# The down stage of a SwiGLU kernel takes its memory where gate/up leaves it, and starts loading inside the last gate/up product group

## The chip, the cores and the metric

The kernel runs on one core of one Trainium2 chip. The number that counts is the device time of one execution in microseconds (us). Inside the core TensorE (PE in the profile) multiplies matrices, VectorE (DVE) and ScalarE (ACT) do elementwise work, GpSimd (POOL) does elementwise work on SBUF alone, and SyncE (SP) issues all the DMAs named here. Each engine works through its own list of instructions in order and waits on semaphores of the others.

## The reference, cut to what matters

The whole is one layer of a streaming encoder: a mixer (SSD and band attention), then SwiGLU. Only the second half matters here, for 1,024 prompt frames and 32 sample frames, with 1,024 model columns and 2,816 hidden columns.

```
f = rmsnorm(x, norm_ffn_g)
x = x + (silu(f @ w_gate) * (f @ w_up)) @ w_down
```

## The kernel before, in words

All products use operands split into a high and a low float32r part, and three matmuls each (high by high, low by high, high by low). Gate/up and down both use a seven-product form of Strassen's scheme.

**Gate/up** goes over 11 pairs `n` of hidden blocks, and for each pair over gate (`w` = 0) and up (`w` = 1): 22 groups of seven products. `prep` loads two weight blocks `raw` (three buffers in pool `wp`), splits them on ACT and DVE and forms their sums on POOL; the results stand in `whi`/`wlo` (five buffers each). `quad` (L973) runs the seven products into four wide PSUM buffers and adds them into pieces of one large SBUF tile `sc`; its helper `product` (L963) issues 24 matmuls (L970). The B operands are `fA` (first and third product) and five tiles `T2, T1, T3, B22, T4` of pool `tq`. `use_up` (L999) multiplies up by the silu of gate and stores the 32 sample columns to `asm_d` in DRAM (L1003); `keep_acts` (L1019) stores the hidden activations to `act_d` in DRAM: seven operands, each split on ACT (L1012) and DVE (L1013) into two pieces that are used in turn, two stores each (L1015).

**Down** has 24 tiles. The first chunk of four tiles uses pair 0 alone, five further chunks use two pairs each (1 and 2, 3 and 4, to 9 and 10). A tile is 128 rows by two halves; it reads its activations (`load_act`, L1049), runs seven products of three matmuls per pair (L1123) and adds each into one of seven accumulators `Z` (L1128). `prep_down` (L1075) prepares one pair's weights: eight small matmuls with the sample activations `asm` (L1079), an add into `x2s`, then splits on ACT (L1091) and DVE (L1092) and sums on POOL (L1096 to L1100) into `chi`/`clo` (three buffers) and `bhi`/`blo` (nine buffers, three per pair). POOL's sums work in place on the raw weights, so they wait for the small matmuls that read these.

The down stage's pool `pd` is opened when gate/up's pools `hp`, `wp` and `tq` are closed, so it lies on their memory. All its loads stand in the program after the last `keep_acts`. The residual x enters as the first value of three accumulators (L1108, 1 MB each) and, in the chunk before the last, by an add on POOL. `load_act(tiles_[m + 2])` stands ahead of tile m, with three two-pair buffers.

The order on each engine is not the order in the source: a scheduler with a time model places each instruction in its engine's list. DMAs on SP use eight completion semaphores in turn, so each also waits for the DMA eight places earlier. What moves is therefore read from the lists.

Of the kernel before, what the change touches and what calls it, by code (L numbers as in the profile page):

```python
# [43 lines left out]
def build(tc, a):  # L44
# [856 lines left out]
    tq = pool("tq", stack=stT)  # L901
# [129 lines left out]
    work = [(w, n) for n in range(NF // 2) for w in range(2)]  # L1031
    ops = prep(*work[0])
    for k, (w, n) in enumerate(work):
        cur, ops = ops, prep(*work[k + 1]) if k + 1 < len(work) else None
        quad(cur, acts if w else gates, use_up(n) if w else use_gate)
        if w:
            keep_acts(n)
    stT.close()
    pvs.close()
    stH.close()  # L1040

    pd = pool("pd")
    pz = pool("pz", space=PSUM)
# [18 lines left out]
    load_raw(0)  # L1065
    load_raw(1)
    asm = pd.tile([P, NF, NS], F32, name="asm")
    nc.sync.dma_start(asm, asm_d)
    Z = pd.tile([P, 7, 4, 512], F32, name="Z")

    def bank1():
        return pz.tile([P, 512], F32, tag="z", bufs=8, name=nm("ps_z"))

    def prep_down(n):

        pb = bank1()
        for k in range(2):
            for g in range(4):
                nc.tensor.matmul(pb[32 * g:32 * g + 32, 0:256], lhsT=asm[:, 2 * n + k, :],  # L1079
# [181 lines left out]
```

## Time and profile before

| what | us |
|---|---|
| median of three runs (lowest, highest) | 1389.52 (1388.25, 1394.1) |
| the profiled execution | 1384.95 |
| its span, first to last instruction | 1383.2 |
| gate/up's last product ends, from the span's start | 1118.86 |
| first matmul of the down stage | 1145.62 |

Rows of stretches give the stretch and its length, then the busy time of each engine with its number of instructions, the clock that was granted to TensorE as a share of full speed, the mean busy share of the DMA engines and what they moved in GB/s. Rows of the chain of waits give start, length and what the chain passed through; the chain is followed back from the last instruction, so what stands in it set the end. A matmul's own duration is longer than the distance to the next, since matmuls are pipelined.

### The profile page before, as it was taken

What the parts mean: (1) busy time and instruction counts of PE and PEld (TensorE: products, weight loads), DVE (VectorE), ACT (ScalarE), POOL (GpSimd) and SP (SyncE); (2) the same over time, 40 slices, a digit from 0 to 9 for tenths busy, and PEclk for the clock granted to TensorE, in tenths of its full rate; (3) what the DMA queues carried; (4) which work ended last, traced back from release to release, by engine and by line L of the source; (5) the groups of instructions that cost most, each with busy time, mean ns of one, the idle gap of its engine ahead of it and who ended that gap; (6) DMA issues with size and microseconds to landing.
All of it is one profiled execution on the core that took longest, in us unless ns stands there. A gap on an engine that the chain in (4) does not pass through costs nothing.

```text
span 1383.2 us, 23748 instructions
## 1 busy us (share of the span) xinstructions
PE 1283.8 (93%) x9260; PEld 1171.9 (85%) x9260; DVE 901.3 (65%) x1271; ACT 502.2 (36%) x865; POOL 600.2 (43%) x495
## 2 busy tenths in 40 slices
PE   5999999878998999997799999999999937999998
PEld 4999999868887788786799999999999935787877
DVE  6356537685757556666777666776766636666896
ACT  7244332322346444544533333333333315111210
POOL 7142258986645101302344435445435315232585
PEclk9999999988999999999999999999999978999999
DMA  7174351445387986654144444554444368766654
GB/s 272 70 229 133 95 177 59 152 161 171 111 255 220 312 266 208 217 172 149 51 138 133 130 145 133 168 154 128 130 144 137 109 197 323 283 224 229 253 187 175
DMA packets 200848, 241.99 MB, mean 175 GB/s; under 512 B 25088, under 2 KB 162368, under 8 KB 200736
## 3 DMA queue, kind: packets, MB, share of 16 engines
q1 hardware_dynamic: 200736, 240.47, 53.2%
q8 instruction: 73, 1.20, 0.4%
q14 instruction: 39, 0.32, 0.1%
HBM read 149.44 MB, written 90.99 MB: 174 GB/s over the span
## 4 chain that ended last, share of the span: by engine, by line
PE 66%; DVE 7%; POOL 6%; issue 6%; DMA 6%; ACT 2%; SPq 1%; DVEq 0%; ACTq 0%; POOLq 0%
PE ps_w L970 32%; PE ps_z L1123 11%; PE ps_mm L153 3%; PE ps_mm L154 3%; PE ps_mm L155 3%; PE ps_mm L162 2%; PE ps_mm L160 2%; PE ps_mm L161 2%; DVE Z L1128 2%; PE ps_mm L734 2%; PE ps_t L717 1%; POOL dm L541 1%; PE ps_s L695 1%; PE ps_s L699 1%; DMA mx<-mix_d 1%
## 5 line engine op out<-in xcount | busy, mean ns | idle before, releaser
L970 PE MATMUL ps_w<-T,whi 128*128 128x264 f32 x1408 | 231.3, 287 | 7.9 <-ACT T L918 7.3
L970 PEld LDWEIGHTS ps_w<-T,whi 128*128 128x128 f32 x1408 | 196.9, 190 | 8.6 <-ACT T L918 7.7
L1123 PE MATMUL ps_z<-bhi,at 128*128 128x512 f32 x528 | 168.2, 393 | 3.9 <-ACT bhi L1091 3.9
L978 DVE TENSOR_TENSOR sc<-sc,ps_w 128x528 f32<-128x528 f32 x154 | 105.4, 698 | 83.3 <-PE ps_w L970 81.0
L153 PE MATMUL ps_mm<-whi,hT_hi 128*128 128x256 f32 (+1 forms) x512 | 149.5, 292 | 5.1 <-ACT hT_hi L227 3.5
L155 PE MATMUL ps_mm<-whi,hT_lo 128*128 128x256 f32 (+1 forms) x512 | 148.9, 291 | 0.5 <-DVE hT_lo L228 0.5
L154 PE MATMUL ps_mm<-wlo,hT_hi 128*128 128x256 f32 (+1 forms) x512 | 148.9, 291 | 0.0
L970 PE MATMUL ps_w<-T,wlo 128*128 128x264 f32 x704 | 144.2, 286 | 0.0
L139 POOL TENSOR_TENSOR wlo<-raw,whi 128x1024 fp32r<-128x1024 f32 (+1 forms) x32 | 80.7, 2531 | 131.5 <-ACT whi L138 130.0
L1128 DVE TENSOR_TENSOR Z<-ps_z,Z 128x512 f32<-128x512 f32 x152 | 101.9, 687 | 44.1 <-PE ps_z L1123 37.4
L1123 PEld LDWEIGHTS ps_z<-bhi,at 128*128 128x128 f32 x528 | 99.5, 189 | 26.3 <-ACT bhi L1091 5.2
L946 ACT CAST whi<-raw 128x1024 fp32r<-128x1024 f32 x88 | 82.9, 944 | 101.6 <-PE ps_w L970 85.2
L970 PE MATMUL ps_w<-fA,whi 128*128 128x264 f32 x704 | 115.6, 287 | 0.0
L947 DVE TENSOR_TENSOR wlo<-raw,whi 128x1024 fp32r<-128x1024 f32 x88 | 107.1, 1218 | 6.0 <-ACT whi L946 3.4
L1013 DVE TENSOR_TENSOR sc<-sc 128x512 fp32r<-128x512 f32 x77 | 74.6, 980 | 54.8 <-DMA act_d<-sc 29.7
L970 PEld LDWEIGHTS ps_w<-T,wlo 128*128 128x128 f32 x704 | 109.8, 190 | 0.0
L153 PEld LDWEIGHTS ps_mm<-whi,hT_hi 128*128 128x128 f32 x512 | 99.8, 195 | 6.8 <-ACT hT_hi L227 3.9
L1123 PE MATMUL ps_z<-blo,at 128*128 128x512 f32 x264 | 103.4, 393 | 1.1 <-DVE blo L1092 1.0
L155 PEld LDWEIGHTS ps_mm<-whi,hT_lo 128*128 128x128 f32 x512 | 99.9, 195 | 1.8 <-DVE hT_lo L228 1.2
L154 PEld LDWEIGHTS ps_mm<-wlo,hT_hi 128*128 128x128 f32 x512 | 99.7, 195 | 0.3
L970 PEld LDWEIGHTS ps_w<-fA,whi 128*128 128x128 f32 x704 | 98.6, 190 | 0.0
L1012 ACT CAST sc<-sc 128x512 fp32r<-128x512 f32 x77 | 46.8, 621 | 122.6 <-DVE sc L1002 77.7
(268 smaller groups left out, 2928.8 us busy)
## 6 DMA issues: line engine op xcount, KB each, us to landing
act_d<-sc SPq DMA_DIRECT2D x154, 256.0 KB, 2.9
at<-act_d SPq DMA_DIRECT2D x20, 1792.0 KB, 7.1
raw<-in_wgu_dram SPq DMA_DIRECT2D x44, 512.0 KB, 3.5
raw<-in_wd_dram SPq DMA_DIRECT2D x22, 512.0 KB, 4.5
x<-in_xp_dram SPq DMA_DIRECT2D x16, 512.0 KB, 6.7
q<-qst_d SPq DMA_DIRECT2D x32, 256.0 KB, 4.8
mx<-mix_d SPq DMA_DIRECT2D x16, 512.0 KB, 4.5
raw<-in_wq_dram SPq DMA_DIRECT2D x14, 512.0 KB, 5.1
```

Source lines behind the costliest of these rows:

```text
L139: (eng or nc.gpsimd).tensor_tensor(lo, raw, hi, op=ALU.subtract)
L153: nc.tensor.matmul(ps_, lhsT=lh, rhs=rh, start=start, stop=False)
L154: nc.tensor.matmul(ps_, lhsT=lh, rhs=rl, start=False, stop=False)
L155: nc.tensor.matmul(ps_, lhsT=ll, rhs=rh, start=False, stop=stop)
L946: nc.scalar.copy(out=t[0][:, 0:w], in_=src)
L947: nc.vector.tensor_tensor(t[1][:, 0:w], src, t[0][:, 0:w], op=ALU.subtract)
L970: nc.tensor.matmul(out[:, h, :], lhsT=A[x][:, kb, :], rhs=B[:, y, kb, h * Q:(h + 1) * Q], start=(n == 0), stop=(n == len(terms) - 1))
L978: add = lambda o, x, y: nc.vector.tensor_tensor(o, x, y, op=ALU.add)
L1012: nc.scalar.copy(out=hi.bitcast(F32R), in_=src)
L1013: nc.vector.tensor_tensor(lo.bitcast(F32R), src, hi, op=ALU.subtract)
L1123: nc.tensor.matmul(pb, lhsT=at[:, k, q, x, :], rhs=bops[n0 + k][name][y], start=(i == 0), stop=(i == len(terms) - 1))
L1128: eng.tensor_tensor(o, x, y, op=ALU.add)
```

## The change

Memory of the down stage is laid into places that gate/up leaves one after another, instead of a pool opened after all of it.

- `tq` moves to the other side of SBUF; `hp` and `wp` stay open to the end. The four activation places are now slices of `fA`, which the last group frees after its third product; a fifth (`at5`) is added after gate/up. A two-pair tile takes two of the five places, each loaded by a DMA of its own.
- Weights of a pair go into the `whi`/`wlo` buffers (five) and into `sd`, which lies on `sc` (four more places). `chi`/`clo` lie in the `raw` buffers of `wp`.
- Pair 0 is loaded and prepared, and its small matmuls run, within the last group of seven products, with a copy of its sample columns in `mixS`. The first four tiles' activations are loaded from the third product of that group on.
- The residual no longer fills three accumulators at the start. The first chunk writes all seven (four products by ACT, three by DVE), and POOL adds the residual later: two per tile in the chunk of pairs 3 and 4, one per tile in the chunk of pairs 5 and 6, and one, as before, in the chunk of pairs 7 and 8.
- `prep_next` places the second pair of a chunk behind the fourth tile of the chunk before; the loads of tile m + 2 stand behind tile m.

```diff
-    tq = pool("tq", stack=stT)
+    tq = pool("tq", stack=stT, side="right")
...
+    fA_f = fA.rearrange("p s k c -> p (s k c)")
+    at_slots = [fA_f[:, k * 4 * H:k * 4 * H + 7 * 2 * P] for k in range(4)]
+    b_slots, c_slots = [], []
+    at_turn, b_turn = [0], [0]
+    asm0 = mixS[:, 0:2, :]
     def load_act(key):
         n0, r, tp = key
-        at = pd.tile([P, r, 7, 2, P], F32R, tag="at", bufs=3, name=nm("at"))
-        nc.sync.dma_start(at.bitcast(F32), act_d[n0:n0 + r, :, tp].rearrange("n p q s c -> p n q s c"))
-        ats[key] = at
-    chunks_ = [(0, 1)] + [(n, 2) for n in range(1, NP, 2)]
-    tiles_ = [(n0, r, tp) for n0, r in chunks_ for tp in range(4)]
-    load_act(tiles_[0])
-    load_act(tiles_[1])
-    def load_raw(n):
-        raws[n] = [pd.tile([P, 1024], F32, tag="raw", bufs=4, name=nm("raw")) for _ in range(2)]
+        ats[key] = []
+        for n in range(n0, n0 + r):
+            at = at_slots[at_turn[0] % len(at_slots)]
+            at_turn[0] += 1
+            nc.sync.dma_start(at.bitcast(F32), act_d[n, :, tp].rearrange("p q s c -> p (q s c)"))
+            ats[key].append(at.rearrange("p (q s c) -> p q s c", q=7, s=2))
...
+    def next_slot():
+        k = b_turn[0]
+        b_turn[0] += 1
+        if k < 5:
+            b_slots.append([wp.tile([P, 1024], F32R, tag=tag, bufs=5, name=nm(tag)) for tag in ("whi", "wlo")])
+        return b_slots[k % 9]
+    def prep_down(n, pb, act):
...
         nc.vector.tensor_tensor(x2s, pb[:, 0:256], x2s, op=ALU.add)
...
-        W = [pd.tile([P, 512], F32R, tag=tag, bufs=3, name=nm(tag)) for tag in ("chi", "clo")]
-        X, V, U = ([pd.tile([P, 1024], F32R, tag=tag, bufs=9, name=nm(tag)) for tag in ("bhi", "blo")]
-                   for _ in range(3))
+        if n < 3:
+            c_slots.append(wp.tile([P, 1024], F32, tag="raw", bufs=3, name=nm("raw")))
+        c = c_slots[n % 3].bitcast(F32R)
+        W = [c[:, 0:512], c[:, 512:1024]]
+        X, V, U = (next_slot() for _ in range(3))
...
+    work = [(w, n) for n in range(NF // 2) for w in range(2)]
+    ops = prep(*work[0])
+    for k, (w, n) in enumerate(work):
+        end = k + 1 == len(work)
+        cur = ops
+        if not end:
+            ops = prep(*work[k + 1])
+            use = use_up(n) if w else use_gate
+        else:
+            load_raw(0, wp, 3)
+            nc.sync.dma_start(asm0, asm_d[:, 0:2])
+            prep_down(0, wide(), asm0)
+            def use(b, h, then=use_up(n)):
+                if b == 0 and h == 0:
+                    for m in range(4):
+                        load_act(tiles_[m])
+                then(b, h)
+        quad(cur, acts if w else gates, use)
+        if w:
+            keep_acts(n)
+    stT.close()
+    pvs.close()
+    pd = pool("pd", side="right")
+    pz = pool("pz", space=PSUM)
+    Z = [pd.tile([P, 4, 512], F32, name=f"Z{k}") for k in range(7)]
+    load_raw(1, pd, 4)
+    load_raw(2, pd, 4)
+    asm = pd.tile([P, NF, NS], F32, name="asm")
+    nc.sync.dma_start(asm, asm_d)
+    at_slots.append(pd.tile([P, 7 * 2 * P], F32R, name="at5"))
+    at_turn[0] = 4
+    sd = hp.tile([P, KB * NT], F32R, tag="lo", name="sd")
+    while len(b_slots) < 5:
+        b_slots.append([wp.tile([P, 1024], F32R, tag=tag, bufs=5, name=nm(tag)) for tag in ("whi", "wlo")])
+    for k in range(4):
+        b_slots.append([sd[:, 2048 * k + 1024 * x:2048 * k + 1024 * (x + 1)] for x in range(2)])
+    def bank1():
+        return pz.tile([P, 512], F32, tag="z", bufs=8, name=nm("ps_z"))
+    def residual(tp, rows, cols, z):
+        x = pd.tile([P, 512], F32, tag="res", bufs=1, name=nm("res"))
+        r0 = 512 * rows + tp * P
+        nc.sync.dma_start(x, xb_d[r0:r0 + P, 512 * cols:512 * cols + 512])
+        nc.gpsimd.tensor_tensor(z, x, z, op=ALU.add)
...
-        if m + 2 < len(tiles_):
-            load_act(tiles_[m + 2])
...
-                if first and i in (1, 5, 6, 7):
+                if first and i in (1, 2, 5, 4):
                     nc.scalar.copy(out=z[i], in_=pb)
+                elif first:
+                    nc.vector.tensor_copy(z[i], pb)
                 else:
                     add(z[i], pb, z[i])
+            if n0 in (3, 5):
+                for i, rows, cols in ((2, 0, 0), (3, 0, 1), (4, 1, 0))[(0 if n0 == 3 else 2):(2 if n0 == 3 else 3)]:
+                    residual(tp, rows, cols, z[i])
...
-                x = pd.tile([P, 512], F32, tag="res", bufs=1, name=nm("res"))
-                nc.sync.dma_start(x, xb_d[512 + tp * P:512 + (tp + 1) * P, 512:1024])
...
-                add(z[7], x, z[7], nc.gpsimd)
+                residual(tp, 1, 1, z[7])
...
-    todo = list(range(1, NP))
+    def prep_next(n):
+        if n < NP:
+            prep_down(n, bank1(), asm[:, 2 * n:2 * n + 2])
+            if n + 2 < NP:
+                load_raw(n + 2, pd, 4)
     for m in range(len(tiles_)):
         n0, r, tp = tiles_[m]
-        ahead = [n for n in todo if n < n0 + r + 2]
-        for n in ahead[:1 if r == 2 else 1]:
-            if tp in ((0, 2) if r == 1 else (2, 3)):
-                todo.remove(n)
-                prep_down(n)
-                if n + 1 < NP and n + 1 not in raws:
-                    load_raw(n + 1)
+        if tp == (0 if r == 1 else 2):
+            prep_next(n0 + r)
+        elif tp == 2:
+            prep_next(n0 + r + 1)
         down_tile(m)
+        if r == 2 and tp == 3:
+            prep_next(n0 + r + 1)
+        for k in {0: (4,), 2: (5,)}.get(m, (m + 2,) if m > 3 else ()):
+            if k < len(tiles_):
+                load_act(tiles_[k])
```

Three places in the engines' lists follow. On TensorE around the start of the last group: `ps_w_12019` is the last product of the group before it, `ps_w_12046` (before) and `ps_w_12080` (changed) are its own first product. Before:

```order
L970 MATMUL ps_w_12019<-T_7218,whi_11598 128x264 x4
L970 MATMUL ps_w_12019<-T_7218,wlo_11599 128x264 x2
L970 MATMUL ps_w_12046<-fA,whi_11839 128x264 [waits DVE_49]
L970 MATMUL ps_w_12046<-fA,whi_11839 128x264 x3
L970 MATMUL ps_w_12046<-fA,wlo_11840 128x264 x2
```

Changed:

```order
L970 MATMUL ps_w_12019<-T_7218,wlo_11599 128x264 x2
L1064 MATMUL ps_w_12051<-raw_12046,mixS 32x256 [waits DMAHW4_49,DMAHW1_49,DVE_49]
L1064 MATMUL ps_w_12051<-raw_12046,mixS 32x256 x3
L1064 MATMUL ps_w_12051<-raw_12047,mixS 32x256 [waits DMAHW1_49]
L1064 MATMUL ps_w_12051<-raw_12047,mixS 32x256 x3
L970 MATMUL ps_w_12080<-fA,whi_11839 128x264 [waits DVE_49,PE_49]
L970 MATMUL ps_w_12080<-fA,whi_11839 128x264 x3
```

Pair 0's eight small matmuls now stand ahead of the last group, and they wait for the two weight blocks `raw_12046` and `raw_12047`.

On SP at the change from gate/up to down. Before, from the last two activation stores on (`asm` is the read of all sample columns):

```order
L1015 DMA act_d<-sc 512x1x128 [waits DMAHW0_49,DVE_49]
L1052 DMA at_12279<-act_d 128x1792 [waits DMAHW1_49,PE_49]
L1052 DMA at_12281<-act_d 128x1792 [waits DMAHW4_49,DMAHW5_49,DMAHW3_49,DMAHW6_49,DMAHW2_49,DMAHW7_49,DMAHW0_49,Pool_49]
L1063 DMA raw_12283<-in_wd_dram 128x1024
L1063 DMA raw_12284<-in_wd_dram 128x1024
L1063 DMA raw_12287<-in_wd_dram 128x1024
L1063 DMA raw_12288<-in_wd_dram 128x1024
L1068 DMA asm<-asm_d 128x704
L1108 DMA Z<-xb_d 128x4x512 [waits PE_49]
```

Changed, from the weights of pairs 1 and 2 on:

```order
L1051 DMA raw_12322<-in_wd_dram 128x1024 [waits DMAHW5_49,PE_49]
L1051 DMA raw_12323<-in_wd_dram 128x1024 [waits DMAHW6_49,PE_49]
L1051 DMA raw_12326<-in_wd_dram 128x1024 [waits DMAHW7_49]
L1051 DMA raw_12327<-in_wd_dram 128x1024 [waits DMAHW0_49]
L1003 DMA asm_d<-sc 128x16 [waits DMAHW1_49,DVE_49]
L1015 DMA act_d<-sc 512x1x128 [waits DMAHW2_49,Activation_49]
L1015 DMA act_d<-sc 512x1x128 [waits DMAHW3_49,Activation_49]
L1015 DMA act_d<-sc 512x1x128 [waits DMAHW4_49,DVE_49]
L1015 DMA act_d<-sc 512x1x128 [waits DMAHW5_49,DVE_49]
L1045 DMA at_12332<-act_d 128x1792 [waits DMAHW6_49]
L1142 DMA res_12880<-xb_d 128x512 [waits DMAHW7_49]
L1127 DMA asm<-asm_d 128x704 [waits DMAHW1_49,DMAHW0_49]
```

The read of the sample columns stood behind all stores, two activation tiles and four weight blocks; it now stands behind four weight blocks, four of the ten last stores, one activation place and one residual block, and six stores follow it.

On TensorE around pair 10, the last: `ps_z_13681` and `ps_z_13720` are its small matmuls, `ps_z_13713` the first product of tile 19, `ps_z_13702` the last of tile 19 and `ps_z_13744` the first of tile 20. Before:

```order
L1079 MATMUL ps_z_13681<-raw_13609,asm 32x256 [waits DMAHW5_49,DVE_49]
L1079 MATMUL ps_z_13681<-raw_13609,asm 32x256 x3
L1079 MATMUL ps_z_13681<-raw_13610,asm 32x256 [waits DMAHW6_49]
L1079 MATMUL ps_z_13681<-raw_13610,asm 32x256 x3
L1123 MATMUL ps_z_13713<-chi_13269,at_13511 128x512 [waits DMAHW7_49,DVE_49]
```

Changed:

```order
L1155 MATMUL ps_z_13702<-sd,fA 128x512 x3
L1064 MATMUL ps_z_13720<-raw_13422,asm 32x256 [waits DMAHW5_49,DVE_49]
L1064 MATMUL ps_z_13720<-raw_13422,asm 32x256 x3
L1064 MATMUL ps_z_13720<-raw_13423,asm 32x256 [waits DMAHW7_49]
L1064 MATMUL ps_z_13720<-raw_13423,asm 32x256 x3
L1155 MATMUL ps_z_13744<-raw_12061,fA 128x512 [waits DMAHW2_49,DVE_49]
```

The second pair's small matmuls have moved from ahead of a chunk's fourth tile to behind it; the same holds for pairs 4, 6 and 8.

## Rows read from the trace of the kernel before

**Rows 1.** The profile page: busy time of each engine over the span

```profile
PE 1283.8 (93%) x9260; PEld 1171.9 (85%) x9260; DVE 901.3 (65%) x1271; ACT 502.2 (36%) x865; POOL 600.2 (43%) x495
```

**Rows 2.** Stretches: last group, gap, first matmuls, most of down, last chunk's start

```profile
1098.20:1118.90 20.70, 20.64 (x169) 20.43 (x168) 8.19 (x13) 2.49 (x4) 0.75 (x1) 1.00 0.18 52
1118.90:1145.60 26.70, 0.00 (x0) 0.01 (x1) 8.59 (x10) 5.27 (x8) 4.98 (x4) 0.55 0.83 283
1145.60:1155.30 9.70, 6.24 (x41) 3.03 (x42) 2.79 (x5) 3.21 (x5) 8.36 (x6) 0.84 1.01 382
1155.30:1295.00 139.70, 139.70 (x681) 110.12 (x682) 96.69 (x130) 33.99 (x44) 43.82 (x29) 0.99 0.67 251
1340.00:1350.00 10.00, 8.43 (x34) 5.68 (x33) 9.54 (x9) 1.86 (x3) 7.57 (x5) 1.00 0.45 175
```

**Rows 3.** The chain of waits across the gap: start, length, what

```profile
1109.92 8.94 PE ps_w L970 x73
...
1136.03 9.45 DMA asm<-asm_d
...
1145.62 1.12 PE ps_z L1079 x8
...
1195.85 9.79 PE ps_z L1123 x42
1205.63 1.00 PE ps_z L1079 x16
```

**Rows 4.** Timeline of TensorE where the last group starts: start, length, instruction

```profile
1098.13 0.65 PE L970 MATMUL ps_w<-fA,whi 128*128 128x264 f32 x4
```

**Rows 5.** Timeline of VectorE: the last reader of the last group's weights

```profile
1096.28 1.23 DVE L947 TENSOR_TENSOR wlo<-raw,whi 128x1024 fp32r<-128x1024 f32 x1 [0.19 <-ACT whi L946]
```

**Rows 6.** Timeline of SyncE's DMA issues in the gap

```profile
1118.04 3.65 SPq L1003 DMA_DIRECT2D asm_d<-sc  x2
1122.01 9.41 SPq L1015 DMA_DIRECT2D act_d<-sc  x10
1131.52 2.54 SPq L1052 DMA_DIRECT2D at<-act_d  x2
...
1136.03 0.61 SPq L1068 DMA_DIRECT2D asm<-asm_d  x1
```

**Rows 7.** DMA issues of 1060 to 1120: count, KB, median us to landing

```profile
raw<-in_wgu_dram SPq DMA_DIRECT2D x1, 512.0 KB, 3.4
asm_d<-sc SPq DMA_DIRECT2D x7, 8.0 KB, 1.6
```

**Rows 8.** DMA issues of 1119 to 1160, the busiest stretch

```profile
Z<-xb_d SPq DMA_DIRECT2D x3, 1024.0 KB, 13.7
```

**Rows 9.** DMA issues of the rest of down

```profile
at<-act_d SPq DMA_DIRECT2D x20, 1792.0 KB, 7.1
...
at<-act_d SPq DMA_DIRECT2D x1, 896.0 KB, 5.0
res<-xb_d SPq DMA_DIRECT2D x3, 256.0 KB, 2.5
```

**Rows 10.** Short stretches of the gap and behind it

```profile
1126.00:1130.00 4.00, 0.00 (x0) 0.00 (x0) 1.39 (x2) 0.89 (x2) 0.00 (x0) 0.50 1.00 286
...
1134.00:1146.00 12.00, 0.38 (x4) 0.23 (x8) 2.52 (x3) 2.28 (x3) 0.00 (x0) 0.50 1.02 400
...
1156.00:1158.00 2.00, 2.00 (x6) 1.51 (x6) 1.64 (x2) 1.73 (x3) 0.19 (x1) 0.50 0.61 198
1158.00:1160.00 2.00, 2.00 (x9) 1.59 (x8) 1.48 (x2) 0.29 (x1) 2.00 (x2) 0.77 0.62 242
```

**Rows 11.** POOL's groups of instructions in down

```profile
L1100 POOL TENSOR_TENSOR raw<-raw,raw 128x512 f32<-128x512 f32 x10 | 21.4, 2143 | 0.0
...
L1128 POOL TENSOR_TENSOR Z<-res,Z 128x512 f32<-128x512 f32 x4 | 6.1, 1516 | 0.0
```

**Rows 12.** Line 1092 on VectorE: shortest, median, longest in ns

```profile
L1092 DVE TENSOR_TENSOR blo<-raw,bhi x33: 1210/1225/2303, 1143.1 to 1347.9; 128x1024 fp32r<-128x1024 f32 x33
```

More of the change, by code (lines that the diff above doesn't have):

```diff
@@ L1029, in keep_acts @@
             keep(n, q, v)
[L1031 to L1046, printed above, removed]
-    ats, raws, bops = {}, {}, {}
+    ats, raws, bops = {}, {}, {}
@@ L1062, in load_raw @@
+    def load_raw(n, pl, bufs):
+        raws[n] = [pl.tile([P, 1024], F32, tag="raw", bufs=bufs, name=nm("raw")) for _ in range(2)]
         for k in range(2):
             nc.sync.dma_start(raws[n][k], a["wd"][2 * n + k])
[L1065 to L1076, printed above, removed]
+    def next_slot():
[4 more added lines that the diff above has]
+        return b_slots[k % 9]
@@ L1077, in prep_down @@
+    def prep_down(n, pb, act):
         for k in range(2):
             for g in range(4):
-                nc.tensor.matmul(pb[32 * g:32 * g + 32, 0:256], lhsT=asm[:, 2 * n + k, :],
+                nc.tensor.matmul(pb[32 * g:32 * g + 32, 0:256], lhsT=act[:, k, :],
                                  rhs=raws[n][k][:, g * 256:(g + 1) * 256], start=(k == 0), stop=(k == 1),
@@ L1084, in prep_down @@
         b11, b12, b21, b22 = r1[:, 0:512], r1[:, 512:1024], r2[:, 0:512], r2[:, 512:1024]
-        W = [pd.tile([P, 512], F32R, tag=tag, bufs=3, name=nm(tag)) for tag in ("chi", "clo")]
-        X, V, U = ([pd.tile([P, 1024], F32R, tag=tag, bufs=9, name=nm(tag)) for tag in ("bhi", "blo")]
-                   for _ in range(3))
+        if n < 3:
[3 more added lines that the diff above has]
+        X, V, U = (next_slot() for _ in range(3))
         def split(t, src):
-            w = src.shape[-1]
-            nc.scalar.copy(out=t[0][:, 0:w], in_=src)
-            nc.vector.tensor_tensor(t[1][:, 0:w], src, t[0][:, 0:w], op=ALU.subtract)
+            nc.scalar.copy(out=t[0], in_=src)
+            nc.vector.tensor_tensor(t[1], src, t[0], op=ALU.subtract)
         split(W, b11)
@@ L1103, in prep_down @@
         bops[n] = dict(B11=op(W, 0), B21=op(X, 0), B22=op(X, 512), T2=op(V, 0), T3=op(V, 512), T4=op(U, 0), T1=op(U, 512))
-    prep_down(0)
-    for z, rows, cols in ((1, 0, 0), (2, 0, 1), (3, 1, 0)):
-        nc.sync.dma_start(Z[:, z], xb_d[512 * rows:512 * rows + 512, 512 * cols:512 * cols + 512]
-                          .rearrange("(t p) c -> p t c", p=P))
+    chunks_ = [(0, 1)] + [(n, 2) for n in range(1, NP, 2)]
+    tiles_ = [(n0, r, tp) for n0, r in chunks_ for tp in range(4)]
+    work = [(w, n) for n in range(NF // 2) for w in range(2)]
[41 more added lines that the diff above has]
+        nc.gpsimd.tensor_tensor(z, x, z, op=ALU.add)
     def down_tile(m):
@@ L1113, in down_tile @@
         first, late, last = n0 == 0, n0 == NP - 4, n0 == NP - 2
-        if m + 2 < len(tiles_):
-            load_act(tiles_[m + 2])
         at = ats.pop(tiles_[m])
-        z = [None] + [Z[:, i, tp, :] for i in range(7)]
+        z = [None] + [Z[i][:, tp, :] for i in range(7)]
         def product(q, name):
@@ L1122, in product @@
             for i, (k, x, y) in enumerate(terms):
-                nc.tensor.matmul(pb, lhsT=at[:, k, q, x, :], rhs=bops[n0 + k][name][y], start=(i == 0),
+                nc.tensor.matmul(pb, lhsT=at[k][:, q, x, :], rhs=bops[n0 + k][name][y], start=(i == 0),
                                  stop=(i == len(terms) - 1))
@@ L1172, in down_tile @@
         store(z[4], 1, 0)
[L1174 removed]
+    def prep_next(n):
[3 more added lines that the diff above has]
+                load_raw(n + 2, pd, 4)
     for m in range(len(tiles_)):
         n0, r, tp = tiles_[m]
[L1178 to L1185 removed]
+        if tp == (0 if r == 1 else 2):
+            prep_next(n0 + r)
+        elif tp == 2:
+            prep_next(n0 + r + 1)
+        down_tile(m)
+        if r == 2 and tp == 3:
[3 more added lines that the diff above has]
+                load_act(tiles_[k])
     nc.sync.dma_start(a["o_ys"], x2s)
+    stH.close()
     top.close()
```

## The prediction, made before the changed kernel ran

> **What bounds the kernel now.** I read the page's head first, then the chain of waits backwards from the end, then stretches of the part that the change touches. TensorE is busy 93% of the span [rows 1], so a gain can only come from the few places where it stands still. In most of the down stage it doesn't: 139.70 of 139.70 us between 1155.3 and 1295 [rows 2]. The largest hole lies between the two stages. The last group's products end at 1109.92 + 8.94 = 1118.86, the first matmul of the down stage starts at 1145.62 [rows 3]: 26.8 us in which TensorE does nothing. The chain says what fills them: seven operands of the last pair are split and stored (ten stores, issued up to 1122.01 + 9.41 = 1131.4 [rows 6]), then loads, and last the read of all sample columns, `asm`, which takes 9.45 us [rows 3]. Behind the hole follow 9.7 us with TensorE busy for 6.24 [rows 2], while pair 0's weights are still being split and summed. So the reader is to see one hole of 26.8 us and a ragged edge of 3.5, and a stage behind them that is bound by TensorE.
>
> **The change part by part.** I follow the path that sets the end; + is a loss.
>
> *Pair 0 ahead of the last group: +3.3.* Its eight small matmuls now stand in TensorE's list ahead of the last group, which started at 1098.13 [rows 4]. The second weight block goes into the buffer of the last group's first block, whose last reader on DVE ends at 1096.28 + 1.23 = 1097.51 [rows 5]. A block lands 3.4 us after its issue here [rows 7]: 1100.9. The first half of the small matmuls fits before that, the second takes half of 1.0 [rows 3]: 1101.4, so the last group starts 3.3 us late. Queued behind the waiting matmuls is the whole group, and behind that everything; nothing covers this. Bounds: +1.0 if the block is there in time (the matmuls alone), +5.0 if the clock also falls. In the large hole it fell to half, 1.2 of 2.4 GHz (mean 0.55 [rows 2]), and a restart then costs 1.5 us, worked out below. Here TensorE idles about 2.3 us; I count no fall.
> The rest of pair 0's preparation (four splits on ACT and four on DVE, four sums on POOL) lies within the group, where DVE is busy 8.19 of 20.70 us, ACT 2.49 and POOL 0.75 [rows 2]. Four DVE splits of at most 1.225 us [rows 12] are under 4.9 us; they fit and I cost them at nothing. If DVE fell behind by one product (the group has four PSUM buffers), it would cost that product's 3 us.
>
> *The hole: 26.8 becomes 14.4, −12.4.* The group ends at 1118.86 + 3.3 = 1122.2. The first down matmuls are now pair 1's small ones, and they wait for the same read of `asm`, which can't be issued before the last `asm_d` store has landed. That store was issued at 1118.04 + 3.65 − 0.33 = 1121.4, 2.5 us behind the last product [rows 6]; now about 1124.7. In SP's list four weight blocks go ahead of it, and four activation stores, one activation place and a residual block go ahead of the read. Their bytes, at 400 GB/s for loads and 286 for these stores [rows 10]: 2.10 MB, 5.2 us; 1.05 MB, 3.7 us; then 0.92 + 0.26 + 0.36 MB, 3.9 us; 12.8 in all, from 1122.2 to 1135.0. Tested on before: two activation tiles, four blocks and `asm`, 4.29 MB from 1131.52 [rows 6], make 10.7 us, and it landed at 1145.49, 3.2 later than that. Some of this is the queue starting from empty, which it does not do now; I add half, 1.6: 1136.6, a hole of 14.4. Bounds: a small read that passed the others would land as a 256 KB residual block does, 2.5 us after its issue [rows 9]: issued at 1126.3 (the store's 1.6 [rows 7]) it lands at 1128.8, 7.8 us earlier; if it takes 9.45 us again, from an issue at 1129, it lands at 1138.5, 1.9 later.
> The row shows a small read held by what was issued ahead of it: 352 KB took 9.45 us [rows 3], 256 KB alone 2.5 [rows 9]. The Trainium skill, "DMA: Bandwidth & Descriptors", section "Queues, rings and completion order", says that a DMA engine takes the descriptors of a ring in ring order. By that rule the weight blocks loaded early speak against the change: the sum is −12.4; without it −20.2.
>
> *The ragged edge: −3.5 − 1.0 − 1.5.* Pair 0's weights and its activations are ready when the first tile comes, so 9.70 − 6.24 = 3.5 us of idling go [rows 2], and so do pair 0's small matmuls there (1.0 [rows 3]; I counted them above). The edge also lets the clock fall a second time: granted 0.50 in 1156 to 1158 and 0.77 in 1158 to 1160 [rows 10], which is 1.0 + 0.5 = 1.5 us of work lost. With one hole instead of a hole and an edge, one fall is left. What is late next there is ACT: its copy of the third product stands behind a split into `sd`, which waits until every activation store has landed, about 5 us after `asm`. Eight PSUM buffers let TensorE run ten products of three matmuls, 10 × 3 × 9.79 / 42 = 7.0 us [rows 3], before it needs that copy. It is covered by 2 us; without the cover each further microsecond counts fully.
>
> *Later preparation of the second pairs: +1.5.* The small matmuls of pairs 4, 6, 8 and 10 come one tile later (9.79 us [rows 3]), and POOL's sums wait for them. At the last chunk's start TensorE already idles 1.57 us of 10 [rows 2]; there POOL and DVE are behind, and I take as much again. At the other three, the list gives TensorE first pair's work, about 34 matmuls or 7.9 us, before it needs the second pair's; two sums, one split on ACT and one on DVE are about 5. Bounds: 0 and 4 × 1.5 = 6.
> At nothing: the residual's adds on POOL (12 more, 1.5 us each [rows 11]) over two chunks, in which POOL has been busy 43.8 of 139.7 us [rows 2]; copies instead of adds in the first chunk; the early read into `mixS`, one wait of SP among stores; the place of `tq`.
>
> Sum: 3.3 − 12.4 − 3.5 − 1.0 − 1.5 + 1.5 = −13.6. The span of 1383.2 becomes 1369.6, the profiled execution 1384.95 − 13.6 = 1371.3; that one ran 4.6 us below the median of the timed runs, 1389.52, from which I forecast 1389.5 − 13.6 = 1375.9.
>
> **Rivals.** *The read is not held* (7.8 us more): 1368.1. For it: it is small and its own wait ends early. Against it: it was held before.
> *The chunk starts eat it:* the second pair's preparation is late at all four starts by some 3.4 us each, no net change, 1389.5. For it: POOL's last sum takes 2.14 us on average, its residual adds 1.5 [rows 11], and twelve more of these now stand between. Against it: the list has more first-pair work there than the sums take.
> A DVE split takes 1.225 us in the median and 2.303 at worst [rows 12]. The Trainium skill, "GPSIMD Engine Reference", section "Specifications", says that GpSimd shares its SBUF access with VectorE, with contention for DVE instructions with two SBUF inputs. By that rule the 12 added adds could each cost one split 1.1 us; the trace agrees that splits are stretched; on DVE's time that is 13 us in two chunks, on the end nothing by my sum and the most of this rival's price if it falls on the chunk starts.
> *Activations come late, and the kernel is slower.* Five one-pair places replace six. The second half of a tile can only be issued when the tile two before it is through, so it has one tile, 9.79 us, to land. The median of today's double loads is 7.1 us, and a single one took 5.0 [rows 9], but the three large loads in the busiest stretch took 13.7 [rows 8]. If each took that, 3.9 us late × 18 tiles = 70 us, 1446. It decides from a landing of 9.79 + 13.6 / 18 = 10.5 us on. Against it: DMA is busy 0.67 there [rows 2], and 3 MB of residual over two chunks add little.
>
> **How the numbers follow.** The forecast 0.80, read not held 0.06, chunk starts 0.08, activations late 0.06. About 0.5%, 7 us, is what can be told from no change here. Faster takes the first two, 0.86; same 0.08; slower 0.06. Low: −13.6 − 7.8 = −21.4, 1368.1. High: 1.9 for the read, 1.5 for the clock and 4.5 for the chunk starts on top, −5.7, 1383.8; that leaves out the two last rivals, 0.14.
>
> **What would show it.** After: the last group starts near 1101.4 with a short wait on a weight block; the hole is 14 us, ended by `asm`; the first tile then runs without a wait on a split; the fully busy stretch goes on, with about 3 us idle near the last chunk's start. It is wrong if the hole is over 20 us, if TensorE waits for `fA` or `at5` in tiles from 5 on, or if it waits at each chunk start.

## The result, and the profile after

| | before | after |
|---|---|---|
| median of five runs, us (lowest, highest) | 1390.49 (1388.25, 1394.1) | 1380.17 (1377.94, 1382.87) |
| ratio to before, with its 95% interval | 1 | 0.9925 [0.9903, 0.9947] |
| profiled execution, span | 1384.95, 1383.2 | 1378.53, 1376.8 |
| gate/up's last product ends | 1118.86 | 1122.42 |
| first matmul of the down stage | 1145.62 | 1138.18 |

The change makes the kernel 10.3 us faster, between 7.4 and 13.5. Of all runs of this document one, of the first of the three combinations below, took 2492.01 us in the slow state and is in no ratio. The two profiled spans differ by 6.4 only; where the rest is comes below. First TensorE's share on the page, then stretches of the kernel after (the columns are those of [rows 2]).

```profile
PE 1289.9 (94%) x9260; PEld 1175.1 (85%) x9260; DVE 905.5 (66%) x1271; ACT 503.0 (37%) x865; POOL 613.3 (45%) x507
```

```profile
1098.00:1102.00 4.00, 4.00 (x41) 3.27 (x40) 3.02 (x4) 3.25 (x5) 0.56 (x1) 1.00 0.29 117
1123.00:1138.00 15.00, 0.00 (x0) 0.00 (x0) 8.13 (x9) 4.65 (x7) 4.27 (x3) 0.65 1.03 341
1138.00:1145.00 7.00, 6.82 (x29) 4.60 (x30) 3.11 (x5) 3.38 (x5) 5.47 (x4) 0.54 0.56 164
1145.60:1155.30 9.70, 9.70 (x55) 7.31 (x54) 6.89 (x9) 4.92 (x9) 2.96 (x3) 1.00 0.74 249
1155.30:1295.00 139.70, 139.32 (x671) 109.68 (x670) 93.23 (x125) 28.75 (x35) 56.05 (x39) 1.00 0.67 242
1330.00:1335.00 5.00, 2.70 (x11) 1.72 (x10) 5.00 (x7) 0.00 (x0) 3.77 (x3) 1.00 0.31 84
1335.00:1340.00 5.00, 5.00 (x16) 3.71 (x15) 2.26 (x3) 0.00 (x0) 5.00 (x5) 0.66 1.00 374
1340.00:1345.00 5.00, 3.35 (x14) 2.14 (x13) 2.49 (x3) 1.53 (x2) 5.00 (x4) 1.00 0.45 175
```

They answer to [rows 2]: the ragged edge behind 1145.6 is gone (9.70 of 9.70), the long stretch is full but for 0.4 us, and the start of the last chunk, which lost 1.57 us before, now loses 2.30 + 1.65 = 3.95 us, with the clock lowered in between (0.66 on average). The hole on TensorE's timeline and the issue of the read that ends it on SyncE's:

```profile
1138.18 1.94 PE L1064 MATMUL ps_z<-raw,asm 128*32 128x256 f32 x16 [15.79 <-DMA asm<-asm_d]
```

```profile
1131.27 0.38 SPq L1127 DMA_DIRECT2D asm<-asm_d  x1
```

The hole is 15.8 us where it was 26.8 [rows 3]. The chain of waits after, at the last chunk's start (start, length, what):

```profile
1333.51 1.14 DVE wlo L1078
1334.69 3.95 PE ps_z L1155 x10
1338.65 1.28 POOL Z L1160
1339.94 1.26 POOL raw L1083
1341.22 1.05 ACT whi L1077
1342.29 1.24 DVE wlo L1078
1343.58 25.00 PE ps_z L1155 x108
```

Here pair 10's preparation sets the end: its first split on DVE, its sums on POOL (with a sum of another tile between them), its next split on ACT and DVE, and only then TensorE's last 108 matmuls.

### The profile page after: what moved, and what is told of

It is laid out like the page before. It is cut to its first block, busy times and chain, and to the rows that moved or that the text cites. A ratio compares the mean times of both kernels' runs of the same rounds, so it can differ in the third digit from the quotient of the medians.

```text
span 1376.8 us, 23827 instructions
## 1 busy us (share of the span) xinstructions
PE 1289.9 (94%) x9260; PEld 1175.1 (85%) x9260; DVE 905.5 (66%) x1271; ACT 503.0 (37%) x865; POOL 613.3 (45%) x507
## 4 chain that ended last, share of the span: by engine, by line
PE 65%; issue 10%; POOL 8%; DVE 7%; DMA 6%; ACT 2%; SPq 0%; POOLq 0%; ACTq 0%; DVEq 0%
PE ps_w L970 33%; PE ps_z L1155 5%; PE ps_mm L153 4%; PE ps_mm L154 4%; PE ps_mm L155 4%; DVE Z L1160 2%; PE ps_mm L160 2%; PE ps_mm L162 2%; PE ps_mm L161 2%; DMA res<-xb_d 2%; PE ps_mm L734 2%; PE ps_t L717 1%; PE ps_s L695 1%; DMA mix_d<-ot 1%; POOL dm L541 1%
## 5 line engine op out<-in xcount | busy, mean ns | idle before, releaser
L1160 DVE TENSOR_TENSOR Z<-ps_z,Z 128x512 f32<-128x512 f32 x140 | 92.3, 685 | 33.9 <-PE ps_z L1155 30.2
L1155 PE MATMUL ps_z<-whi,fA 128*128 128x512 f32 x276 | 99.6, 400 | 3.2 <-DVE Z L1160 1.7
L954 POOL TENSOR_TENSOR raw<-raw,raw 128x512 f32<-128x512 f32 x22 | 37.1, 1687 | 90.8 <-DVE wlo L947 90.8
L970 PE MATMUL ps_w<-fA,wlo 128*128 128x264 f32 x352 | 72.4, 288 | 0.0
```

Of the source, the lines that this page charges most:

```text
L970: nc.tensor.matmul(out[:, h, :], lhsT=A[x][:, kb, :], rhs=B[:, y, kb, h * Q:(h + 1) * Q], start=(n == 0), stop=(n == len(terms) - 1))
L1155: nc.tensor.matmul(pb, lhsT=at[k][:, q, x, :], rhs=bops[n0 + k][name][y], start=(i == 0), stop=(i == len(terms) - 1))
L1160: eng.tensor_tensor(o, x, y, op=ALU.add)
```

## The experiments

All are edits of the changed kernel (the first is none) and are timed against the kernel before, to which the changed kernel stands at 0.9925. What a run tells of one place is read from its profile, since an interval of 0.2% is 3 us. "Lost to the clock" is busy time times the missing share of the clock, summed over stretches of one us. The late chunk is that of pairs 7 and 8, the last but one. The first experiment and the one on the fifth activation place ran once each and have no ratio.

**The kernel before, once more.** No edit.

> The kernel before once more, for a second profile of it. In its first profile the first matmul of gate/up starts at 655.2 us; in the profiles of the changed kernel and of its four variants so far at 658.7 to 660.0, though nothing ahead of that is changed. Theory (an execution differs by some us in the first half, and the first profile of before was a quick one): this profile starts gate/up later, between 657 and 661, and its span is 2 to 6 us above 1383.2. Rival (the change delays the first half through where its memory lies): 655 again, span near 1383.

The first matmul of gate/up on TensorE's timeline in the first profile of before, in the second, and after:

```profile
655.22 1.23 PE L970 MATMUL ps_w<-fA,whi 128*128 128x264 f32 x4
```

```profile
661.97 1.23 PE L970 MATMUL ps_w<-fA,whi 128*128 128x264 f32 x4
```

```profile
659.42 1.23 PE L970 MATMUL ps_w<-fA,whi 128*128 128x264 f32 x4
```

The second span is 1387.4, 4.2 above the first. The same kernel begins gate/up 6.8 us later in another execution; the theory holds, though 661.97 lies 1 us above its range. So 4.2 us of the distance between the two profiles that are compared here lie ahead of everything that was changed.

**Pair 0's small matmuls inside the last group.**

```diff
-            prep_down(0, wide(), asm0)
             def use(b, h, then=use_up(n)):
                 if b == 0 and h == 0:
+                    prep_down(0, wide(), asm0)
```

> The changed kernel, but pair 0's small matmuls stand behind the third product of the last group and not ahead of the group. Theory (the group starts 3.6 us late because TensorE waits for a weight block in front of it): the group starts near 1098.2 without a wait and its last matmul ends 2.3 to 2.6 us earlier (the 1.0 us of small matmuls stays); 2 us off the whole if the hole behind it keeps its length. Rival (the hole ends at a time set by the transfers, not by TensorE): the group ends earlier, the first down matmul starts where it did, and the time does not change.

Ratio 0.9944 [0.9924, 0.9964]. TensorE's timeline: the small matmuls and the first down matmul.

```profile
1109.63 1.07 PE L1064 MATMUL ps_w<-raw,mixS 128*32 128x256 f32 x16
...
1138.60 1.94 PE L1064 MATMUL ps_z<-raw,asm 128*32 128x256 f32 x16 [15.96 <-DMA asm<-asm_d]
```

From gate/up's first matmul to the start of its last it is 462.43 us here and 462.69 after: nothing is won. Neither expectation names the reason: there was no wait. Between 1098 and 1102 TensorE of the kernel after is busy for 4.00 of 4.00 us, so the weight block had landed; the small matmuls cost their own 1.0 wherever they stand.

**Pair 2's weight blocks behind the read.** Two blocks, 1.05 MB, wait until `asm` has landed.

```diff
-    def load_raw(n, pl, bufs):
+    def load_raw(n, pl, bufs, behind=None):
...
+        for r in raws[n] if behind is not None else ():
+            nc.gpsimd.tensor_copy(r[:, 0:1], behind)
...
-    load_raw(2, pd, 4)
     nc.sync.dma_start(asm, asm_d)
+    load_raw(2, pd, 4, asm[:, NF - 1, 0:1])
```

> The changed kernel, but pair 2's two weight blocks (1.05 MB) are asked for only after asm has landed (a copy of one column on GpSimd makes their transfers wait). Theory (the small read waits for the bytes issued ahead of it): asm lands 1.05 MB / 400 GB/s = 2.6 us earlier, the hole is 13.2 us instead of 15.8, and the time falls by 2 to 3 us. Rival 1 (the read takes its 7 us whatever stands ahead of it, and its issue decides): the hole is 15 to 16 us. Rival 2: the stores behind it get slower by the blocks that now come among them, and the gain is lost at the second product of pair 2; no change in the time.

The read among the DMA issues (count, KB, median us to landing), of 1119 to 1140 after and of 1119 to 1136 here, and where the hole ends here:

```profile
asm<-asm_d SPq DMA_DIRECT2D x1, 352.0 KB, 6.7
```

```profile
asm<-asm_d SPq DMA_DIRECT2D x1, 352.0 KB, 3.8
```

```profile
1133.98 1.94 PE L1066 MATMUL ps_z<-raw,asm 128*32 128x256 f32 x16 [12.08 <-DMA asm<-asm_d]
```

The read lands 2.9 us sooner after its issue, 2.6 were expected; the hole is 12.1. Rival 1, that the read takes its 7 us whatever stands ahead of it, falls. But the scheduler also placed the activation place and the residual block ahead of the four stores here (issued at 1122.4 and 1122.9; after, at 1128.7 and 1130.7), so the 2.9 us are not sure to be the two blocks' alone. The ratio is 0.9926 [0.9904, 0.9947], no gain: in this profile TensorE lost 3.15 us waiting for `fA` near 1248, and 1.7 us to the clock behind that. The experiment with two residual buffers deals with such a wait.

**Sample columns for pairs 1 and 2 read early.**

```diff
-    asm0 = mixS[:, 0:2, :]
+    asm0 = mixS[:, 0:6, :]
...
-            nc.sync.dma_start(asm0, asm_d[:, 0:2])
+            nc.sync.dma_start(asm0, asm_d[:, 0:6])
...
-            prep_down(n, bank1(), asm[:, 2 * n:2 * n + 2])
+            prep_down(n, bank1(), (asm0 if n < 3 else asm)[:, 2 * n:2 * n + 2])
```

> The changed kernel, but the small matmuls of pairs 1 and 2 take their sample columns from mixS, where columns 0 to 5 are read before the last group, so nothing at the start of the down stage waits for asm. Theory (the read of asm, held behind 4.7 MB, ends the hole): the hole now ends when pair 1's first weight block has landed, 1126.2 in the profile after; it shrinks from 15.8 us to about 4, and the kernel runs about 10 us faster than the changed one, 0.985 of the kernel before. Rival 1 (the stores of the last activations are as late as the read): a new stall of 4 to 10 us opens at the start of the first chunk of two pairs, because the splits into sd wait for these stores; the time is then 0.988 to 0.993 of before. Rival 2 (something else ends the hole): the hole stays over 12 us.

Ratio 0.9878 [0.9858, 0.9899]. TensorE behind the last group, and ACT where pair 2's splits stand:

```profile
1126.26 1.02 PE L1064 MATMUL ps_z<-raw,mixS 128*32 128x256 f32 x8 [3.31 <-DMA raw<-in_wd_dram]
```

```profile
1152.51 2.94 ACT L1077 CAST sd<-raw 128x1024 fp32r<-128x1024 f32 x3 [2.08 <-DMA act_d<-sc]
```

The hole is 3.3 us and ends with pair 1's first weight block, as the theory has it; 12.5 us go there. Rival 1 is there too, but small: ACT waits 2.08 us for the last activation store, and TensorE loses 1.0. By the ratios the time fell by 6.5 us and not by 10; by the two profiles it fell by 10.2 (1378.53 and 1368.31, the quickest of its six runs), and intervals of 3 us each don't tell 6.5 from 10. In this profile 1.8 us were lost near 1240 to 1246, of them 1.4 in a wait for `fA`.

**Two buffers for a residual block.**

```diff
-        x = pd.tile([P, 512], F32, tag="res", bufs=1, name=nm("res"))
+        x = pd.tile([P, 512], F32, tag="res", bufs=2, name=nm("res"))
```

> The changed kernel with two buffers for a residual block instead of one. In the profile after, two residual loads sit 6.5 us in SP's list (1240.9 to 1247.4) because their one buffer waits for GpSimd, and the load of the next activations stands behind them; TensorE then waits 0.2 us for these activations there, and 0.9 to 3.1 us in the profiles of the three experiments run so far that keep this part. Theory (the residual's buffer holds SP's queue, and through it the activations): with two buffers the activation load goes out at 1242 or earlier, TensorE does not wait for fA between 1240 and 1260, the stretch is 0 us idle; the time is 1 to 3 us less. Rival (the load is late because of the bytes ahead of it): TensorE still waits there 0.2 to 3 us.

SyncE's issues in the kernel after, where the wait arises:

```profile
1236.62 0.86 SPq L1045 DMA_DIRECT2D fA<-act_d  x2
1240.90 6.53 SPq L1142 DMA_DIRECT2D res<-xb_d  x2
1247.47 0.43 SPq L1045 DMA_DIRECT2D fA<-act_d  x1
```

POOL's waits for residual blocks (us in total, times, longest) after, from 1200 to 1250, and with two buffers, in the same 50 us 3 us earlier:

```profile
POOL Z L1143 <- DMA res<-xb_d: 17.9, 5, 4.9
```

```profile
POOL Z L1143 <- DMA res<-xb_d: 3.0, 1, 3.0
```

TensorE's stretch 1240 to 1260 with two buffers, where the kernel after had 19.62 of 20:

```profile
1240.00:1260.00 20.00, 20.00 (x100) 15.90 (x99) 14.11 (x19) 2.68 (x3) 10.44 (x6) 1.00 0.73 263
```

The theory holds: POOL waits 3.0 us for residual blocks where it waited 17.9, and TensorE is not idle there. Measured from pair 6's small matmuls (1243.46 after, 1240.57 here) the activation load goes out 0.6 us ahead of them and not 4.0 behind. Ratio 0.9912 [0.9885, 0.9938], 1.8 us better than after, which the intervals alone would not show.

**The last residual block in the chunk of pairs 1 and 2.** In this kernel the block flows through z1 into one more block of the output, so that it doesn't compute the layer; the number of loads and adds is the same.

```diff
+            if n0 == 1:
+                residual(tp, 1, 1, z[7])
...
-                residual(tp, 1, 1, z[7])
```

> The changed kernel, but the last residual block (into z7) is added in the chunk of pairs 1 and 2, where GpSimd is idle, and not in the late chunk; four GpSimd adds of 1.3 to 1.8 us leave the stretch 1286 to 1340. Theory (in the late chunk DVE falls behind, since its adds of two SBUF operands take 1.3 us beside a busy GpSimd, so pair 10's preparation ends late): TensorE's idle time between 1325 and 1346 falls from 3.9 us to 2 or less, the clock does not fall there (1.7 us), and the time falls by 3 to 4 us. Rival (DVE's own load and the list's order decide, GpSimd does not): idle time 3 to 4 us as before, the time unchanged within 1 us.

**One of DVE's four sums to GpSimd.**

```diff
-                add(z[7], z[5], z[7])
+                add(z[7], z[5], z[7], nc.gpsimd)
```

> The changed kernel, but one of the four sums that DVE makes for each tile of the late chunk (z7 + z5) is made by GpSimd: four adds of 1.31 us leave DVE there, four of some 1.55 us come to GpSimd. Theory (DVE is full in the late chunk, 40.5 of 41.0 us, and the splits of pair 10 stand behind its adds): DVE gets 5 us of room, TensorE is idle 2 us or less between 1325 and 1346 instead of 3.9, the clock does not fall there, and the time falls by 2 to 4 us. Rival (GpSimd's own list, 31.7 of 41 us and in order, makes pair 10 late): its sums come later by up to 6 us, TensorE is idle 4 to 8 us there, and the time does not fall or rises.

**Ten places for split operands**, with the early columns.

```diff
-        return b_slots[k % 9]
+        return b_slots[k % 10]
...
+    b_slots.append([pd.tile([P, 1024], F32R, name="xhi"), fA_f[:, 4 * 7 * 2 * P:4 * 7 * 2 * P + 1024]])
```

> The changed kernel with columns 0 to 5 read early, and ten places for split operands in place of nine (the tenth in the rest of fA and in 4 KB more of the pool; the activation places in fA lie close together), so that pair 10's first split takes a place that pair 6 left and not pair 7. One residual buffer. Theory (pair 10 is late in the last chunk because its splits can't begin before the late chunk's last tile and then queue behind DVE's adds): its first split comes some 8 us earlier, TensorE is idle 2 us or less in the 20 us behind the start of the last chunk (3.9 us in the experiment with early columns alone) and the clock does not fall there; time 2 to 4 us below that experiment, 0.985 to 0.986 of before. Rival (DVE and GpSimd are full in the late chunk, and order alone gains nothing): idle 3 to 5 us there, time 0.988.

The start of the last chunk in four kernels: after, residual early, sum on GpSimd, ten places.

```profile
1328.00:1348.00 20.00, 16.05 (x60) 11.54 (x59) 12.76 (x16) 3.17 (x4) 17.03 (x11) 0.91 0.47 171
```

```profile
1325.00:1345.00 20.00, 16.89 (x80) 11.63 (x79) 13.13 (x17) 3.98 (x5) 13.90 (x10) 1.00 0.44 157
```

```profile
1325.00:1351.00 26.00, 21.21 (x89) 15.37 (x89) 16.07 (x21) 5.16 (x6) 26.00 (x18) 0.87 0.40 143
```

```profile
1318.00:1338.00 20.00, 15.59 (x58) 11.35 (x57) 10.55 (x15) 2.58 (x3) 16.13 (x12) 0.91 0.45 173
```

TensorE is idle 3.95, 3.1, 4.8 and 4.4 us there. Four adds fewer on POOL help by 0.8 us and the clock stays up (1.00, where 1.7 us were lost to it), but the idle time is the rival's 3 to 4 us and not the theory's 2; four sums more on POOL, with DVE relieved by as many, make it worse, POOL being busy for 26.00 of 26.00. With ten places pair 10's first wide split on DVE (X in `prep_down`) starts 22.6 us ahead of its small matmuls (1291.82 and 1314.39) where it started 7.2 behind them (1333.43 and 1326.28), and the idle time doesn't shrink. POOL's timeline with ten places shows why:

```profile
1316.81 1.68 POOL L1161 TENSOR_TENSOR Z<-Z,Z 128x512 f32<-128x512 f32 x1 [1.23 <-DVE Z L1161]
1318.44 1.83 POOL L1144 TENSOR_TENSOR Z<-res,Z 128x512 f32<-128x512 f32 x1
1321.50 1.68 POOL L1161 TENSOR_TENSOR Z<-Z,Z 128x512 f32<-128x512 f32 x1 [1.23 <-DVE Z L1161]
1323.13 1.30 POOL L1082 TENSOR_TENSOR raw<-raw,raw 128x512 f32<-128x512 f32 x1
```

Pair 10's first sum (the last row) has all its operands when the small matmuls end, at 1315.5, and starts at 1323.13: ahead of it in POOL's list stand sums of the late chunk, two of which wait for DVE. Ratios: 0.9938 [0.992, 0.9956], 0.995 [0.9929, 0.9972], 0.9851 [0.9826, 0.9876] (early columns alone: 0.9878). So the first two are no faster than the changed kernel. The third ratio is what its theory forecast, but the place that the theory meant has gained nothing: that is luck, or noise, since the intervals of 0.9851 and 0.9878 overlap. My theory, that DVE's queue alone makes pair 10 late, falls; each of the two lists does.

**The fifth activation place at another address.**

```diff
+    at5 = pd.tile([P, 7 * 2 * P], F32R, name="at5")
     Z = [pd.tile([P, 4, 512], F32, name=f"Z{k}") for k in range(7)]
...
-    at_slots.append(pd.tile([P, 7 * 2 * P], F32R, name="at5"))
+    at_slots.append(at5)
```

> The changed kernel with the fifth activation place (at5) taken first in its pool, so that it lies at another address and everything else in that pool is shifted by 7 KB; the instructions and their order are the same. In the profile after, matmuls of 512 columns follow each other every 233 to 234 ns where their stationary operand comes from at5 and every 227 to 228 where it comes from fA; at before all were at 227. Theory (the address of the stationary operand makes the difference): the interval at at5 goes to 227 to 228. Rival (it is something else about these tiles, such as the transfers that run then): it stays at 233.

TensorE's groups of matmuls from `at5` after, then here; a product of six, three from `at5` and three from `fA`, begins with each row:

```profile
1267.23 0.86 PE L1155 MATMUL ps_z<-sd,at 128*128 128x512 f32 x3
...
1268.62 0.86 PE L1155 MATMUL ps_z<-sd,at 128*128 128x512 f32 x3
```

```profile
1268.33 0.86 PE L1156 MATMUL ps_z<-sd,at 128*128 128x512 f32 x3
...
1269.72 0.86 PE L1156 MATMUL ps_z<-sd,at 128*128 128x512 f32 x3
```

1.39 us for six, 232 ns each, in both; the rival. Elsewhere eight matmuls from `fA` take 1.98 us from start to end and one 0.39, so they follow at 1.59 / 7 = 227 ns. What makes the difference stays open.

**Three combinations.** The first joins the early columns with two residual buffers. The second is ten places with the residual asked for from GpSimd's queue:

```diff
-        nc.sync.dma_start(x, xb_d[r0:r0 + P, 512 * cols:512 * cols + 512])
+        nc.gpsimd.dma_start(x, xb_d[r0:r0 + P, 512 * cols:512 * cols + 512])
```

The third is the first with the last residual add moved from the late chunk to the last one:

```diff
-                residual(tp, 1, 1, z[7])
...
         add(z[7], p7, z[7])
+        residual(tp, 1, 1, z[7])
```

> The changed kernel with both edits that have helped alone: columns 0 to 5 read early into mixS (hole 3.3 us instead of 15.8) and two buffers for a residual block (no wait for fA near 1250). Theory (the two places are apart, so their gains add): the hole is 3 to 4 us, TensorE is not idle at the start of the chunk of pairs 5 and 6, and the time is 0.9878 x 0.9912 / 0.9925 = 0.9865 of the kernel before, 1369 to 1371. Rival (what is won early is lost at the last chunk, because DVE and GpSimd are no faster there): TensorE's idle time before the last chunk grows from 4 to 6 us or more, and the time stays at 0.988 or above.

> The same with ten places, and the residual blocks asked for from GpSimd's own queue instead of SP's. Theory (SP's queue was held by residual loads that wait for GpSimd; a load in GpSimd's own list holds nobody else): no wait for fA near the start of the chunk of pairs 5 and 6, 1 to 3 us less than with ten places alone, 0.983 to 0.985 of before. Rival (each issue costs GpSimd's time, and GpSimd, 32 of 41 us busy in the late chunk, gets later): more than 3 us idle before the last chunk, time equal or higher.

> The kernel with early columns and two residual buffers, and the last residual block (into z7) now added by GpSimd in the last chunk, behind z7's last product, and not in the late chunk. Theory (what is late before the last chunk is GpSimd's list: between pair 10's four sums stand sums of the late chunk and residual adds of 1.3 to 2.3 us): four adds leave GpSimd ahead of the last chunk, TensorE's idle time in the 20 us behind the start of the last chunk falls from 2.8 to 2 us or less and the clock does not fall there (1.7 us); 2 to 3 us less than the kernel without this edit, 0.980 to 0.981 of before. Rival 1 (DVE's list decides, not GpSimd's): 2.5 to 4 us idle, same time. Rival 2 (the adds come back at the end, where four stores wait for them): the end of the program is 1 to 4 us later behind the last matmul.

Ratios: 0.9824 [0.9796, 0.9852] (median 1365.99, of five), 0.9867 [0.9843, 0.9892] (1370.45), 0.9847 [0.982, 0.9874] (1367.19). The first has both gains: hole 3.5 us, no idling from 1240 to 1262. It is faster than either edit alone, and by 0.4% more than the sum of 0.9865 that the theory gave; where that comes from is not shown, its one profile being of the slowest of the five. Pair 2's splits into `sd` now cost 2.8 us at the start of its chunk, so rival 1 of the early columns comes back. GpSimd's own queue for the residual is no better than ten places alone (0.9851): the wait for `fA` is gone, as its theory has it, but TensorE is idle 4.4 us at the last chunk's start, as its rival has it. TensorE's waits at the last chunk in the first and in the third:

```profile
PE ps_z L1155 <- DVE wlo L1078: 1.8, 2, 1.6
PE ps_z L1155 <- ACT sd L1077: 1.0, 1, 1.0
```

```profile
PE ps_z L1155 <- DVE wlo L1078: 2.1, 1, 2.1
```

The second wait goes when four residual adds leave POOL's list, the first does not: there are two limits there, DVE's list for the first wide split and POOL's for the sums. The idle time falls from 2.8 to 2.1 us, near the theory's 2; but the clock fell in both, the end comes 0.6 us later behind the last matmul, and the times can't be told apart.

## Why the prediction was right or wrong

1375.9 was forecast, 1380.17 measured, inside the range; the hole and the ragged edge, which make the gain, held. Most of the other terms were mis-sized, and it is luck that two of them, pair 0 (2.3 us too dear) and the last chunk (2.6 too cheap), nearly cancel. By steps, in us, predicted and read from the two profiles:

| step | predicted | read |
|---|---|---|
| pair 0 ahead of the last group | +3.3 | +1.0 |
| the hole | −12.4 | −11.0 |
| idling at the ragged edge | −3.5 | −3.4 |
| small matmuls there | −1.0 | −1.0 |
| the clock at the restart | −1.5 | 0.0 |
| last chunk's start: idle, clock | +1.5 | +2.4, +1.7 |
| residual at nothing | 0 | +0.4 |
| matmuls from `at5` | 0 | +1.8 |
| sum | −13.6 | −8.1 |
| first half; gate/up ahead of its last group | | +4.2, −1.6 |

−5.5 of the 6.5 by which the last matmul ends earlier (1379.15 and 1372.64) are so accounted for; the last 1.0 stays open. The first half is a difference between executions. Gate/up ahead of its last group took 442.9 us in the first profile of before, 442.1 in the second and 441.3 after (without the small matmuls), so most of its −1.6 may be one too. The timed −10.3 is a difference of medians of five; −8.1 lies within its interval.

*Pair 0 ahead of the last group.* The failed step is "the last group starts 3.3 us late". It does start late, by 3.6 in the profile, and the number looks confirmed; but only the 1.0 of small matmuls belongs to the change, which was the lower bound. The rest is the first half, as the second profile of before shows, and the experiment inside the group has nothing to win. The wait was hung on the wrong reader. After, VectorE's last two splits of the last group's weights, then SyncE's issue of pair 0's second block:

```profile
1094.96 1.66 DVE L947 TENSOR_TENSOR wlo<-raw,whi 128x1024 fp32r<-128x1024 f32 x1
...
1098.89 1.23 DVE L947 TENSOR_TENSOR wlo<-raw,whi 128x1024 fp32r<-128x1024 f32 x1 [0.31 <-ACT whi L946]
```

```profile
1096.68 0.34 SPq L1051 DMA_DIRECT2D raw<-in_wd_dram  x1
```

The split of [rows 5], of the group's first block, is the one at 1098.89. The load goes out 2.2 us before that starts and 0.06 behind the other, of the group's second block: it is that block's place which comes free. Pair 0's blocks took 3.4 to 3.9 us to land, so the second was there by 1100.6, and TensorE came to it at 1100.69.

*The hole.* The mechanism is borne out by two runs: bytes taken from ahead of the read make it land sooner, and without the read the hole ends at the next block. The sum over bytes was 1.4 us short (a hole of 14.4 forecast, 15.8 measured), within its bound of 1.9. The Trainium skill, "DMA: Bandwidth & Descriptors", section "Queues, rings and completion order", states the ring order that the prediction leaned on; 6.7 us with and 3.8 without 1.05 MB ahead agree with it.

*The clock.* The second fall went with the edge, as forecast. But the step "a restart then costs 1.5 us" failed: the restart that is left took 3.1 us (6.82 us busy at 0.54 of the clock), as much as the two of before together (3.2), so nothing was saved. In the second profile of before there was one fall only, of 2.6, and in the profiles of this document the restart behind the hole took from 1.5 to 3.1 us. The prediction's 1.5 is the low end; what a restart costs differs by execution, so this term can't be held to the change.

*The last chunk.* The step "later preparation of the second pairs, +1.5" named the place and mis-sized it: 2.4 us more idling, and then a fall of the clock that the sum did not count for so short a wait. Both profiles of before idle 1.5 to 1.6 there without a fall. DVE falls behind as [rows 12] warned. In the kernel after, DVE and POOL side by side:

```profile
1323.32 1.78 DVE L1160 TENSOR_TENSOR Z<-Z,Z 128x512 f32<-128x512 f32 x1
...
1326.95 0.68 DVE L1160 TENSOR_TENSOR Z<-Z,Z 128x512 f32<-128x512 f32 x1
...
1333.43 1.21 DVE L1078 TENSOR_TENSOR wlo<-raw,whi 128x1024 fp32r<-128x1024 f32 x1
```

```profile
1322.28 2.28 POOL L1160 TENSOR_TENSOR Z<-Z,Z 128x512 f32<-128x512 f32 x1
1325.19 1.28 POOL L1160 TENSOR_TENSOR Z<-Z,Z 128x512 f32<-128x512 f32 x1 [0.63 <-DVE Z L1160]
1328.90 1.67 POOL L1160 TENSOR_TENSOR Z<-Z,Z 128x512 f32<-128x512 f32 x1 [2.43 <-DVE Z L1160]
```

The same add takes 1.78 us beside a busy POOL and 0.68 where POOL idles (1326.5 to 1328.9). The Trainium skill, "GPSIMD Engine Reference", section "Specifications", states this contention for two SBUF inputs, and the trace agrees. Pair 10's split, whose ACT half was done at 1325.35, comes at 1333.43 behind such adds.

*At nothing: the residual.* The failed words are "the residual's adds on POOL", costed at nothing. The adds cost TensorE nothing that the profile shows; the wait that comes with them does. A load into the one buffer waits on SP for POOL, and the next activations stand behind it. After shows 0.4 us at that chunk's start; the other profiles with one buffer on SP's queue lost 1.1 to 3.2, in three of them with 1.7 of clock. That is the place of the rival "activations late" and, with the last chunk, of "the chunk starts eat it"; neither reached its price. By the letter the prediction's own sign of being wrong is there, a wait for `fA` in a tile from 5 on, but of 0.2 us.

*`at5`.* Unforeseen. From pair 3's to pair 5's small matmuls it is 1181.90 to 1222.96 = 41.06 us after, and 40.61 before (1205.57 to 1246.18, pairs 4 to 6). The table takes 0.4 in each of four and a half chunks; the next two read 0.8 (without 0.4 of idling) and 0.4. That the tiles with `at5` are the cause rests on their slower products, and why these are slower stays open.

## What to carry to other kernels

Two loads that waited for their buffer held the loads behind them in SyncE's list for 6.5 us here, so their cost stood in another tile's operands; give a small prefetch two buffers before calling it free. When a stage starts with a small read of late data, split off what was ready long ago: here two pairs' columns, read early, took 12.5 us out of a hole that had kept 15.8. A shift seen in two profiles belongs to the change only if it starts behind the first changed instruction; take a second profile of the old kernel.

## What the runs showed of the hardware

Matmuls of 512 columns followed each other at 227 ns where the stationary operand came from `fA` and at 232 to 234 in products that used `at5`, at both of two addresses in the pool; why is not shown. And 2.3 us of idling between 1331.9 and 1335 in the kernel after were followed by three microseconds at the lower of the clock's two levels, 1.2 GHz, while 2.07 us in one piece (from 1332.95, residual early) were followed by none and 1.62 us (1329.1 to 1330.7, two residual buffers) by three again: the length of the idling alone did not decide.
